# S5 state products alternate over two PSUM rings; tap table stored without gaps from ScalarE's queue

## Chip, core and metric

One core of a Trainium2 chip (trn2) runs the whole program in one launch. The metric is the device time in microseconds; before the change its median over three runs is 2743.06 us (2741.53 to 2747.41). Lower is better.

## What is computed

A two-layer encoder trunk over x of 1 x 1024 x 1024 (time x channels), all in float32. Layer 0 mixes time with RWKV-7, layer 1 with S5, a diagonal complex state space of 64 groups of 16 channels; a squared-ReLU MLP (1024 to 4096 to 1024) follows each, and every sub-layer ends in a layer norm. The part that the change touches is S5:

```python
def s5_mix(x, a_re, a_im, log_dt, b_re, b_im, c_re, c_im, d_skip, w_glu):
    ...
        pr, pi, sr, si = lax.associative_scan(combine, (a_ch_re, a_ch_im, bu_re, bu_im), axis=0)
        carry_re, carry_im = cmul(pr, pi, h_re[None], h_im[None])
        s_re = sr + carry_re
        s_im = si + carry_im
        y = (jnp.einsum('tbgp,gcp->tbgc', s_re, cr_w)
             - jnp.einsum('tbgp,gcp->tbgc', s_im, ci_w))
    ...
    y = jax.nn.gelu(y).astype(x.dtype)
    z = y @ w_glu
    return z[..., :d] * jax.nn.sigmoid(z[..., d:])
```

## The kernel before

Channels lie on partitions (8 tiles of 128), time on the free axis, in two halves of 512 steps, A (time 0 to 511) and B. While one half goes through a mixer, whose work is spread over all engines, the other half's MLP or projections keep PE full: dense products of 128 x 512 (line 188, tile d), three for each weight tile because a float32 weight is split into two reduced parts, whi (ScalarE, line 148) and wlo (VectorE, line 149). A weight block wraw comes by DMA on SyncE's queue (line 169) into two buffers, whi and wlo have three each; one block feeds 12 dense products. A scheduler orders the instructions of each engine by rank and a simulated timeline; on the chip each engine takes them strictly in that order. It also gives every DMA one of eight completion semaphores, in turn and over all queues, so that a DMA whose semaphore is still in use by an earlier one waits for that one to land.

S5 runs in steps of 8 time points. s5_tables (line 1029 on) builds three tables in DRAM, channel tile f by channel tile: tB and tC (input and output of the states), and tT, the taps, by which the 8 inputs of a step act on its 8 outputs directly. For tT, PE makes pk (line 1151), ScalarE copies it into kpad behind eight rows of zeros (line 1155), and SyncE stores eight shifted windows of kpad as one DMA for each parity of the groups (line 1159). kpad's innermost index is the group, so tT's columns have a step of four elements.

s5(H, h) (line 1175 on) then turns each pair f2 of channel tiles (u, pbu), lets VectorE and GpSimd carry the states (advance, hb), and forms the output. For a tile pair it loads tt and tcm for both tiles into four buffers that it shares with tb (lines 1240, 1242), and for each parity of the groups it makes 8 tap products (line 1250: 128 rows, 64 output columns of the array, 128 moving columns) and then 16 state products (line 1255: 64 rows, 64 columns, the two tiles j side by side), all into one bank py of the ring "c" (two buffers):

```python
for par in range(2):
    qs = slice(64 * par, 64 * par + 64)
    p = pc.tile([128, HT], F32, tag="c", name="py").rearrange("p (g n) -> p g n", g=4)
    ...
    S.copy(y1[:, :, :, par].rearrange("p t g c -> p g t c"), p.rearrange("p g (t c) -> p g t c", t=SL))
```

ScalarE copies py to y1 (line 1257), PE turns y1 back (pyt, line 1263, ring "a", two buffers), VectorE adds the skip term (line 1265), ScalarE takes GELU (line 1267) and SyncE stores s_y (line 1268), which the GLU reads again as yl (line 946).

Of the kernel before, what the change touches and what calls it, by code (L numbers as in the profile page):

```python
# [8 lines left out]
F32 = mybir.dt.float32  # L9
# [9 lines left out]
HT = 512  # L19
KT = 8  # L20
# [11 lines left out]
LNT = (2, 5)  # L32
TB = 2
LN8R = 400000
MIXR = 100
# [35 lines left out]
def trunk(ctx, tc, A):  # L71
    nc = tc.nc
    V, S, G, PE, SP = nc.vector, nc.scalar, nc.gpsimd, nc.tensor, nc.sync

    cp = ctx.enter_context(tc.tile_pool(name="cp", bufs=1))
    dr = ctx.enter_context(tc.tile_pool(name="dr", bufs=1, space=DRAM))
# [4 lines left out]
    pl = ctx.enter_context(tc.tile_pool(name="pl", bufs=1, space=PSUM))  # L81
# [80 lines left out]
    def wload(src, kt, n, key=None):  # L162
# [3 lines left out]
        for k0 in range(0, kt, step):  # L166
# [14 lines left out]
            out += [(hi[:, k], lo[:, k]) for k in range(step)]  # L181
        return out

    bulk, hops = [], []
# [835 lines left out]
    SL = 8  # L1020
    NSC = HT // SL
    tT = dr.tile([KT, 128, 2, 512], F32, name="tT")
    tB = dr.tile([KT, 128, 4, 2, 128], F32, name="tB")
    tC = dr.tile([KT, 128, 4, 2, 128], F32, name="tC")

    def s5_tables():
        n = [0]
# [76 lines left out]

        kpad = pp.tile([128, 16, 16, 4], F32, name="kpad")
        G.memset(kpad, 0.0)
        for f in range(KT):
            gs = slice(4 * f, 4 * f + 4)
            bc = pp.tile([128, 2, 2, 4, 16], F32, tag="bc", name="bc", bufs=1)
            SP.dma_start(bc, A["s5bc"][f])  # L1110
# [42 lines left out]
            for par in range(2):  # L1153
                ps_ = slice(64 * par, 64 * par + 16)
                S.copy(kpad[ps_, 8:].rearrange("p t c g -> p g (t c)"), p[ps_])
            tv = tT[f].rearrange("(s c) two n -> two c s n", c=16)
            for par in range(2):
                src = kpad[64 * par : 64 * par + 16, 1:9].rearrange("p t c g -> p (t c g)")
                SP.dma_start(tv[par], bass.AP(src.tensor, src.offset, [src.ap[0], (64, SL), src.ap[1]]))

# [12 lines left out]
    def s5(H, h):  # L1173
# [61 lines left out]
        for f2 in range(4):  # L1235
            y1 = s5p.tile([128, SL, 4, 2, 16], F32, tag="u1", name="y1", bufs=2)
            tabs = []
            for f in (2 * f2, 2 * f2 + 1):
                tt = s5p.tile([128, 2, 512], F32, tag="tab", name="tt", bufs=4)
                SP.dma_start(tt, tT[f])  # L1240
                tcm = s5p.tile([128, 4, 2, 128], F32, tag="tab", name="tcm", bufs=4)
                SP.dma_start(tcm, tC[f])
                tabs.append((f, tt.rearrange("p two (n g) -> p two g n", g=4), tcm))
            for par in range(2):
                qs = slice(64 * par, 64 * par + 64)
                p = pc.tile([128, HT], F32, tag="c", name="py").rearrange("p (g n) -> p g n", g=4)

                for g2 in range(4):
                    for j, (f, tv, tcm) in enumerate(tabs):
                        PE.matmul(p[64 * j : 64 * j + 64, g2], ug[f][:, 2 * g2 + par], tv[:, par, g2],  # L1250
                                  start=g2 == 0, stop=False, skip_group_check=True)
                for g2 in range(4):
                    for ri in range(2):
                        for j, (f, tv, tcm) in enumerate(tabs):
                            PE.matmul(p[64 * j : 64 * j + 64, g2], hb[qs, 4 * f + g2, ri, 0:NSC], tcm[qs, g2, ri],  # L1255
                                      start=False, stop=ri == 1, skip_group_check=True)
                S.copy(y1[:, :, :, par].rearrange("p t g c -> p g t c"), p.rearrange("p g (t c) -> p g t c", t=SL))
            for j in range(2):
                f = 2 * f2 + j
                js = slice(64 * j, 64 * j + 64)  # L1260
                p = pa.tile([128, SL, NSC], F32, tag="a", name="pyt")
                for t in range(SL):
# [133 lines left out]
```

## Time and profile before

| | |
|---|---|
| median of 3 runs | 2743.06 us |
| the profiled execution's own time | 2746.6 us |
| its span | 2744.8 us |
| mean granted TensorE clock | 0.961 of full speed |
| PE / PEld busy | 95% / 76% |
| DVE / ACT / POOL busy | 66% / 42% / 23% |
| chain that ended last | PE 44%, of it line 188 39%; lines 1250 and 1255 1% each |
| S5 tables | about 1100 to 1275 us |
| S5 output of half A / half B | about 1481 to 1540 us / 2010 to 2072 us |

The span is the profiler's time from the first to the last instruction; the execution's own time has the start and the end around it. A busy PE is one with products in flight: products overlap, so what one costs is read from the starts of a group and of the next one, not from its length. Each float32 product here leaves two records in the trace, a dense one of line 188 leaves one.

### The profile page before, as it was taken

Reading aid. Unit: us, or ns where it says so; the run is one execution under the profiler, and the core shown is the slowest. Engines: PE = TensorE matmul, PEld = TensorE weight load, DVE = VectorE, ACT = ScalarE, POOL = GpSimd, SP = SyncE. Lnnn points to the kernel's source line nnn. Section 1 sums busy time; section 2 is a strip of 40 time slices with the busy share of each in tenths; the row PEclk is TensorE's granted clock in tenths of the full one; section 3 lists DMA queues with packets and bytes.
Section 4 is the critical chain, followed back from the end, with each engine's and each line's share of the span. In section 5 each row is a group of like instructions: output and inputs, shape, how many; then the busy total and the mean of one; then the engine's idle time right before and its main releaser. Section 6 shows DMA issues by size and latency. Waiting matters only on the chain.

```text
span 2744.8 us, 43807 instructions
## 1 busy us (share of the span) xinstructions
PE 2598.4 (95%) x16582; PEld 2089.9 (76%) x16582; DVE 1813.3 (66%) x3191; ACT 1154.8 (42%) x2038; POOL 630.6 (23%) x515
## 2 busy tenths in 40 slices
PE   7999979989899999989999999999999999999997
PEld 5778757678677777767876788778778887788886
DVE  7477677577786867997567553674855546755556
ACT  7455574544543333353532332434223324433334
POOL 3121542432442122342122000120220101210101
PEclk9989979999899999999999999999999999999998
DMA  4765455564223334545333533233343322333333
GB/s 146 235 214 175 151 164 156 178 203 142 81 86 88 93 92 148 141 129 163 100 112 127 174 95 100 81 96 112 103 164 110 96 96 81 119 96 96 96 96 100
DMA packets 215058, 345.90 MB, mean 126 GB/s; under 512 B 21184, under 2 KB 75584, under 8 KB 214848
## 3 DMA queue, kind: packets, MB, share of 16 engines
q1 hardware_dynamic: 214848, 343.10, 40.5%
q8 instruction: 131, 2.15, 0.3%
q14 instruction: 79, 0.65, 0.1%
HBM read 279.06 MB, written 63.96 MB: 125 GB/s over the span
## 4 chain that ended last, share of the span: by engine, by line
PE 44%; DVE 4%; issue 3%; DMA 1%; POOL 1%; ACT 1%; ACTq 0%; SPq 0%; DVEq 0%; POOLq 0%
PE d L188 39%; PE py L1250 1%; PE py L1255 1%; DVE wlo L149 1%; DMA wraw<-in_mw_dram 1%; PE pu L154 1%; PE pbu L1206 1%; POOL rl L975 1%; DVE hA L991 0%; DMA s_y<-yg 0%; DVE t L1218 0%; DVE hB L991 0%; ACT whi L148 0%; DVE sq L876 0%; PE pu L1195 0%
## 5 line engine op out<-in xcount | busy, mean ns | idle before, releaser
L148 ACT CAST whi<-wraw 128x512 fp32r<-128x512 f32 x668 | 413.5, 620 | 929.1 <-PE d L188 623.2
L149 DVE TENSOR_TENSOR wlo<-wraw,whi 128x512 fp32r<-128x512 f32 x668 | 500.6, 750 | 426.8 <-ACT whi L148 404.3
L188 PE MATMUL d<-qbuf,whi 128*128 128x512 f32 (+1 forms) x2112 | 657.0, 394 | 23.8 <-DVE hA L991 12.8
L188 PEld LDWEIGHTS d<-qbuf,whi 128*128 128x128 f32 x2112 | 391.8, 191 | 120.0 <-DVE hA L991 17.8
L188 PE MATMUL d<-qbuf,wlo 128*128 128x512 f32 (+1 forms) x1056 | 411.9, 392 | 10.7 <-DVE wlo L149 10.4
L975 POOL TENSOR_TENSOR rl<-rl 128x512 f32<-128x512 f32 x128 | 157.2, 1228 | 1094.5 <-ACT rl L974 1094.5
L188 PE MATMUL d<-oAh,whi 128*128 128x512 f32 (+1 forms) x960 | 390.9, 411 | 15.5 <-ACT ev L418 6.3
L188 PE MATMUL d<-oAl,whi 128*128 128x512 f32 (+1 forms) x960 | 387.5, 405 | 3.0 <-DVE oAl L149 2.8
L188 PE MATMUL d<-oAh,wlo 128*128 128x512 f32 (+1 forms) x960 | 386.5, 405 | 2.4 <-DVE wlo L149 2.3
L188 PE MATMUL d<-oBh,whi 128*128 128x512 f32 x704 | 279.2, 397 | 0.0
L188 PE MATMUL d<-oBh,wlo 128*128 128x512 f32 x704 | 278.7, 396 | 0.2 <-DVE wlo L149 0.2
L188 PE MATMUL d<-oBl,whi 128*128 128x512 f32 x704 | 277.1, 394 | 0.0
L188 PEld LDWEIGHTS d<-qbuf,wlo 128*128 128x128 f32 x1056 | 201.7, 191 | 56.5 <-DVE wlo L149 14.5
L188 PEld LDWEIGHTS d<-oAh,whi 128*128 128x128 f32 (+1 forms) x960 | 185.9, 194 | 62.2 <-ACT ev L418 8.4
L188 PEld LDWEIGHTS d<-oAh,wlo 128*128 128x128 f32 (+1 forms) x960 | 185.8, 194 | 44.4 <-DVE wlo L149 3.2
L188 PEld LDWEIGHTS d<-oAl,whi 128*128 128x128 f32 (+1 forms) x960 | 185.6, 194 | 43.1 <-DVE oAl L149 5.2
L991 DVE TENSOR_TENSOR hB<-hB,d 128x512 f32<-128x512 f32 (+1 forms) x256 | 165.0, 650 | 71.2 <-PE d L188 68.0
L991 DVE TENSOR_TENSOR hA<-hA,d 128x512 f32<-128x512 f32 x240 | 162.1, 682 | 64.4 <-PE d L188 62.1
L188 PEld LDWEIGHTS d<-oBh,wlo 128*128 128x128 f32 x704 | 132.9, 189 | 32.4 <-issue 2.0
L188 PEld LDWEIGHTS d<-oBl,whi 128*128 128x128 f32 x704 | 133.1, 189 | 29.9 <-issue 0.7
L188 PEld LDWEIGHTS d<-oBh,whi 128*128 128x128 f32 x704 | 133.1, 189 | 29.0 <-issue 1.2
L149 DVE TENSOR_TENSOR qbuf<-rl,qbuf 128x512 fp32r<-128x512 f32 x128 | 95.0, 742 | 73.5 <-ACT qbuf L148 73.5
(374 smaller groups left out, 3804.8 us busy)
## 6 DMA issues: line engine op xcount, KB each, us to landing
wraw<-in_mw_dram SPq DMA_DIRECT2D x520, 256.0 KB, 2.7
wraw<-in_glu_dram SPq DMA_DIRECT2D x64, 256.0 KB, 2.7
low<-wlo SPq DMA_DIRECT2D x52, 256.0 KB, 2.6
wlo<-low SPq DMA_DIRECT2D x52, 256.0 KB, 3.6
wraw<-in_wk_dram SPq DMA_DIRECT2D x32, 256.0 KB, 3.5
wraw<-in_wr_dram SPq DMA_DIRECT2D x32, 256.0 KB, 3.9
wraw<-in_wv_dram SPq DMA_DIRECT2D x32, 256.0 KB, 4.3
yl<-s_y SPq DMA_DIRECT2D x32, 256.0 KB, 3.1
```

The lines of the kernel that those rows point to most:

```text
L148: S.copy(hi, src)
L149: (e or V).tensor_sub(lo, src, hi.bitcast(F32))
L154: PE.matmul(out, x, idt, start=True, stop=True)
L188: bulk.append((PE.matmul(p, w, x, **kw).ins, x.shape[-1]))
L975: G.tensor_mul(r, r, r)
L991: V.tensor_add(z, z, p)
L1206: PE.matmul(p[qs, g2, ri], tb[:, g2, ri, qs], u[:, 2 * g2 + par], start=True, stop=True)
L1250: PE.matmul(p[64 * j : 64 * j + 64, g2], ug[f][:, 2 * g2 + par], tv[:, par, g2], start=g2 == 0, stop=False, skip_group_check=True)
L1255: PE.matmul(p[64 * j : 64 * j + 64, g2], hb[qs, 4 * f + g2, ri, 0:NSC], tcm[qs, g2, ri], start=False, stop=ri == 1, skip_group_check=True)
```

## The change

Tap products: all of a tile pair come first, into two banks, one for each parity (ring "c" and ring "a"). State products: the order is now group, part, tile j, parity, and a chain of order-only dependences (inorder) holds it, so that four products in a row use four different quarters of the array and the two parities write different banks. pyt moves to the ring "l" with one buffer. The taps are kept with the time and channel index innermost, in DRAM as well (tT by partition first), so that the table is read without a step. kpad becomes two buffers of four tiles each; after every fourth tile ScalarE's queue starts sixteen stores, one for each of eight time shifts and each parity, whose runs are 128 elements long in kpad and 2048 in DRAM; SyncE's two stores per tile are gone.

```diff
+    def inorder(prods):
+
+        for x, y in zip(prods, prods[1:]):
+            tc.add_manual_dep(y.ins, x.ins.name, mybir.DependencyInfo(
+                mybir.DependencyClass.NoSync, mybir.DependencyReason.DATA), reason="order")
...
-    tT = dr.tile([KT, 128, 2, 512], F32, name="tT")
+    tT = dr.tile([128, 2, KT, 4, 128], F32, name="tT")
...
-        kpad = pp.tile([128, 16, 16, 4], F32, name="kpad")
-        G.memset(kpad, 0.0)
+        kpads = [pp.tile([128, TBF, 4, 16, 16], F32, name=f"kpad{j}") for j in range(KT // TBF)]
+        for kpad in kpads:
+            G.memset(kpad[:, :, :, 0:8], 0.0)
...
-                S.copy(kpad[ps_, 8:].rearrange("p t c g -> p g (t c)"), p[ps_])
-            tv = tT[f].rearrange("(s c) two n -> two c s n", c=16)
-            for par in range(2):
-                src = kpad[64 * par : 64 * par + 16, 1:9].rearrange("p t c g -> p (t c g)")
-                SP.dma_start(tv[par], bass.AP(src.tensor, src.offset, [src.ap[0], (64, SL), src.ap[1]]))
+                S.copy(kpad[ps_, f % TBF, :, 8:].rearrange("p g t c -> p g (t c)"), p[ps_])
+            if f % TBF == TBF - 1:
+                for par in range(2):
+                    for s in range(SL):
+                        S.dma_start(
+                            tT[16 * s : 16 * s + 16, par, f - TBF + 1 : f + 1].rearrange("c f g n -> c (f g) n"),
+                            kpad[64 * par : 64 * par + 16, :, :, 1 + s : 9 + s].rearrange("c f g t e -> c (f g) (t e)"))
...
-                SP.dma_start(tt, tT[f])
+                SP.dma_start(tt.rearrange("p two (g n) -> p two g n", g=4), tT[:, :, f])
...
-                tabs.append((f, tt.rearrange("p two (n g) -> p two g n", g=4), tcm))
+                tabs.append((f, tt.rearrange("p two (g n) -> p two g n", g=4), tcm))
+
+
+            pp = [r.tile([128, HT], F32, tag=t, name="py").rearrange("p (g n) -> p g n", g=4)
+                  for r, t in ((pc, "c"), (pa, "a"))]
+            for g2 in range(4):
+                for par in range(2):
+                    for j, (f, tv, tcm) in enumerate(tabs):
+                        PE.matmul(pp[par][64 * j : 64 * j + 64, g2], ug[f][:, 2 * g2 + par], tv[:, par, g2],
+                                  start=g2 == 0, stop=False, skip_group_check=True)
+            prods = []
+            for g2 in range(4):
+                for ri in range(2):
+                    for j, (f, tv, tcm) in enumerate(tabs):
+                        for par in range(2):
+                            qs = slice(64 * par, 64 * par + 64)
+                            prods.append(PE.matmul(pp[par][64 * j : 64 * j + 64, g2], hb[qs, 4 * f + g2, ri, 0:NSC],
+                                                   tcm[qs, g2, ri], start=False, stop=ri == 1, skip_group_check=True))
+            inorder(prods)
...
-                p = pa.tile([128, SL, NSC], F32, tag="a", name="pyt")
+                p = pl.tile([128, HT], F32, tag="l", name="pyt").rearrange("p (t n) -> p t n", t=SL)
```

On PE, in the S5 output of half A, the second tile pair stood so before (py<-tt are tap products, py<-tcm state products, pyt the transposes of the pair before; the first py<-tt row is already in this order in front of them):

```order
L1250 MATMUL py<-tt,ug 64x128
L1263 MATMUL pyt<-ident,y_13883 128x64 x16
L1250 MATMUL py<-tt,ug 64x128 x7
L1255 MATMUL py<-tcm,hb 64x128 x16
L1250 MATMUL py<-tt,ug 64x128 x8
L1255 MATMUL py<-tcm,hb 64x128 x16
L188 MATMUL d<-oBh,whi 128x512
```

and in the changed kernel so (line numbers of the changed file):

```order
L1280 MATMUL pyt<-ident,y_13901 128x64 x8
L195 MATMUL d<-qbuf,whi 128x512 x2
L195 MATMUL d<-qbuf,wlo 128x512
L195 MATMUL d<-qbuf,whi 128x512
L1262 MATMUL py<-tt,ug 64x128 x14
L1270 MATMUL py<-tcm,hb 64x128
L1280 MATMUL pyt<-ident,y_13901 128x64 x8
L1270 MATMUL py<-tcm,hb 64x128 x31
L1262 MATMUL py<-tt,ug 64x128 x2
L195 MATMUL d<-qbuf,whi 128x512
```

The transposes are in two pieces with the taps between them, and the last two py<-tt belong to the third tile pair: they moved from behind some 24 dense products to the place straight behind this pair's state products. The third pair ends the same way, and half B has the same order.

On ACT, where the last tile's tables are built, this stood before:

```order
L1155 COPY kpad<-pk 16x4x128 x2
L1167 COPY bs<-pb_13342 128x512
L148 CAST whi<-wraw 128x512
L974 ACTIVATE rl<-d 128x512
L148 CAST qbuf<-rl 128x512
L148 CAST whi<-wraw 128x512
L1167 COPY bs<-pb_13348 128x512
L148 CAST whi<-wraw 128x512 x9
```

and now:

```order
L1164 COPY kpad_12866<-pk 16x4x128 x2
L1178 COPY bs<-pb_13360 128x512
L1168 DMA tT<-kpad_12866 16x16x128 x16
L1178 COPY bs<-pb_13366 128x512
L981 ACTIVATE rl<-d 128x512
L149 CAST whi<-wraw 128x512 x2
L149 CAST qbuf<-rl 128x512
L149 CAST whi<-wraw 128x512 x9
```

The sixteen stores stand ahead of one bs copy, one ReLU and all further casts. The fourth tile has the same block of sixteen behind its kpad copies and one cast, ahead of two bs copies and two casts.

## Rows read from the trace of the kernel before

**Rows 1.** The page, part 1: busy time, share of the span, instructions.
```profile
PE 2598.4 (95%) x16582; PEld 2089.9 (76%) x16582; DVE 1813.3 (66%) x3191; ACT 1154.8 (42%) x2038; POOL 630.6 (23%) x515
```

**Rows 2.** Stretches: length; busy us of PE, PEld, DVE, ACT, POOL; clock; DMA share; GB/s.
```profile
1260.00:1280.00 20.00, 19.88 (x114) 15.64 (x113) 15.15 (x25) 8.91 (x14) 2.28 (x2) 1.00 0.66 187
1500.00:1540.00 40.00, 40.00 (x321) 29.94 (x320) 17.97 (x25) 14.48 (x25) 2.09 (x2) 1.00 0.70 246
```

**Rows 3.** Timeline of PE, second tile pair: start us, length us, instruction, count.
```profile
1490.55 2.01 PE L1250 MATMUL py<-tt,ug 128*64 128x128 f32 x14
1492.49 1.96 PE L1255 MATMUL py<-tcm,hb 64*64 64x128 f32 x32
1494.38 2.01 PE L1250 MATMUL py<-tt,ug 128*64 128x128 f32 x16
1496.33 1.96 PE L1255 MATMUL py<-tcm,hb 64*64 64x128 f32 x32
1498.22 0.51 PE L188 MATMUL d<-oBh,whi 128*128 128x512 f32 x1
```

**Rows 4.** Timeline of PE, the products pbu of one channel tile.
```profile
1343.73 2.09 PE L1206 MATMUL pbu<-ug,tb 128*64 128x64 f32 x64
1345.74 0.50 PE L188 MATMUL d<-oBl,whi 128*128 128x512 f32 x1
```

**Rows 5.** Stretches of 0.30 us, line 1255 alone: length, PE busy (records), clock, DMA.
```profile
1482.20:1482.50 0.30, 0.30 (x10) 1.00 0.73 273
1482.88:1483.18 0.30, 0.30 (x16) 1.00 0.20 48
1483.70:1484.00 0.30, 0.30 (x10) 1.00 0.75 273
```

**Rows 6.** Tile py: records, ns min/median/max, first and last start, forms.
```profile
L1255 PE MATMUL py<-tcm,hb x512: 269/269/473, 1481.2 to 2057.2; 64*64 64x128 f32 x171
...
L1250 PE MATMUL py<-tt,ug x256: 388/406/422, 1401.4 to 2055.1; 128*64 128x128 f32 x128
```

**Rows 7.** Timelines of SP and PE, and tile tt: request, next tap product, landing.
```profile
1496.42 0.32 SPq L1240 DMA_DIRECT2D tt<-tT  x1
...
1503.26 0.65 PE L1250 MATMUL py<-tt,ug 128*64 128x128 f32 x2
...
DMA to landing us min/median/max: 3.8/4.2/6.2
```

**Rows 8.** Timelines of PE, DVE and SP: from the transposes to the store of y.
```profile
1489.60 1.01 PE L1263 MATMUL pyt<-ident,y 64*128 64x64 f32 x16
...
1490.35 1.17 DVE L1265 SCALAR_TENSOR_TENSOR yg<-hA,pv,pyt 128x512 f32<-128x512 f32 x1
...
1492.21 0.33 SPq L1268 DMA_DIRECT2D s_y<-yg  x1
```

**Rows 9.** Tile kpad: copies, stores in SP's queue, landing; and SP's timeline.
```profile
L1155 ACT COPY kpad<-pk x16: 1055/1074/1087, 1126.9 to 1267.7; 16x512 f32<-16x512 f32 x16
L1159 SPq DMA_DIRECT2D tT<-kpad x16: 320/362/1264, 1128.6 to 1268.9; - x16
...
DMA to landing us min/median/max: 3.9/4.7/5.8
...
1268.48 0.86 SPq L1159 DMA_DIRECT2D tT<-kpad  x2
```

**Rows 10.** Timelines of ACT and PE at the last tile's tables.
```profile
1268.76 0.59 ACT L1167 COPY bs<-pb 128x512 f32<-128x512 f32 x1
1269.53 0.62 ACT L148 CAST whi<-wraw 128x512 fp32r<-128x512 f32 x1 [0.18 <-PE d L188]
...
1275.49 0.62 PE L188 MATMUL d<-qbuf,whi 128*128 128x512 f32 x2
```

**Rows 11.** Timeline of ACT behind the fourth tile's kpad copies; idle time and releaser.
```profile
1175.73 0.62 ACT L148 CAST whi<-wraw 128x512 fp32r<-128x512 f32 x1 [1.61 <-PE d L188]
```

**Rows 12.** Waits of SP's queue, 1060 to 1300 us: total us, times, longest.
```profile
SPq L1159 <- ACT kpad L1155: 12.4, 8, 4.5
```

More of the change, by code (lines that the diff above doesn't have):

```diff
@@ L33 @@
 TB = 2
+TBF = 4
 LN8R = 400000
@@ L1103, in s5_tables @@
         V.tensor_mul(ci, ci, den)
-        kpad = pp.tile([128, 16, 16, 4], F32, name="kpad")
-        G.memset(kpad, 0.0)
+        kpads = [pp.tile([128, TBF, 4, 16, 16], F32, name=f"kpad{j}") for j in range(KT // TBF)]
+        for kpad in kpads:
+            G.memset(kpad[:, :, :, 0:8], 0.0)
         for f in range(KT):
             gs = slice(4 * f, 4 * f + 4)
+            kpad = kpads[f // TBF]
             bc = pp.tile([128, 2, 2, 4, 16], F32, tag="bc", name="bc", bufs=1)
@@ L1239, in s5 @@
                 tt = s5p.tile([128, 2, 512], F32, tag="tab", name="tt", bufs=4)
-                SP.dma_start(tt, tT[f])
+                SP.dma_start(tt.rearrange("p two (g n) -> p two g n", g=4), tT[:, :, f])
                 tcm = s5p.tile([128, 4, 2, 128], F32, tag="tab", name="tcm", bufs=4)
                 SP.dma_start(tcm, tC[f])
-                tabs.append((f, tt.rearrange("p two (n g) -> p two g n", g=4), tcm))
-            for par in range(2):
[L1245 to L1257, printed above, removed]
@@ L1258, in s5 @@
+            inorder(prods)
+            for par in range(2):
+                S.copy(y1[:, :, :, par].rearrange("p t g c -> p g t c"), pp[par].rearrange("p g (t c) -> p g t c", t=SL))
             for j in range(2):
```

## The prediction

> **What bounds the kernel now.** The page's busy times come first: PE is busy for 95% of the span and every other engine far less [rows 1]. The question for any edit is therefore whether it shortens PE's own stream or makes PE wait. The table of stretches says where: in 1500 to 1540 us, inside the S5 output of the first half, PE is busy for all 40 us at the full clock (the 1.00; 2.4 GHz), while DVE has 18.0 us and ACT 14.5 us of work, and the DMA engines are 70% busy with 246 GB/s [rows 2]. There a microsecond less of PE work is a microsecond less of time, unless something PE reads comes later than before. In 1260 to 1280 us, where the last tables are built, PE is busy for 19.88 of 20 us as well [rows 2], so a delay on ACT there is not free.
>
> The timeline of PE inside one pair of channel tiles then gives prices as start-to-start times, which is what counts, because the products overlap: a row's own length (406 or 269 ns each) is not its cost. Eight pairs of tap products (16 records, since each product leaves two) take 1494.38 to 1496.33, 1.95 us; sixteen pairs of state products (32 records) take 1492.49 to 1494.38 and again 1496.33 to 1498.22, 1.89 us each [rows 3]. So a tap pair costs 0.244 us and a state pair 0.118 us, switching included, though both stream 128 columns.
>
> **The change, part by part.**
>
> *Tap products, contiguous table.* They read the moving operand with a step of four elements (16 bytes) before, and without a gap after. The trace has the same tile form without a gap in the products pbu: 128 rows by 64 columns, two at a time, 64 moving columns; 64 records, so 32 pairs, go from 1343.73 to 1345.74, 0.063 us a pair [rows 4]. Twice the columns is 0.126 us, against 0.244. There are 256 records [rows 6], so 128 pairs, in 16 groups of eight: 1.95 less 8 x 0.126 = 0.95 us each, **15.2 us** in all. Bounds: 0, if the step is not why they are slow, and 15.2. I take 15.2, since pbu differs from them in the step and the length alone. The Trainium skill ("SBUF — State Buffer", "Door 1: The DMA port swizzle") says that memory is read in lines of 16 bytes, that full speed wants two hits on a line, and then that one can step freely over "4 fp32". Its first half makes this step slow, its second makes it free; by the second the taps would gain 0 and the sum below would be -2.4 us.
>
> *State products, four in a row.* Before, a parity's 16 pairs run on one half of the array's rows; now the parities alternate, each with a bank of its own. The trace shows four at once by accident: in the first tile pair the two parities' groups follow each other directly, and where the second starts while the first drains, 0.30 us holds 16 records, against 10 in the stretches before and behind it, with records of the same length [rows 5]. 512 records [rows 6] are 16 groups of 1.89 us, 30.2 us; half is 15.1, less about 1 for that overlap, which exists already twice: **14 us**. Bounds: 0 and 15.1. I take 14, because in rows 5 both streams keep their own pace.
>
> *Table loads (a wait added).* All four tables of a tile pair share four buffers, so the next tap table is asked for when the last tap product of this one is done (before: 1496.42, behind the taps that end at about 1496.3) and lands 4.2 us later, 6.2 at most [rows 7]. Before, dense products filled that time and the next tap product started at 1503.26 [rows 7]. Now two tap products of the next pair stand straight behind this pair's state products, at two places in each half, and everything behind them on PE waits with them. Between request and use lie 32 state products (about 1.0 us at four in a row, and some 0.35 us of switching), and half the transposes with their switching (0.8 us): with the tail of the taps about 2.7 us. Wait: 4.2 - 2.7 = 1.5 us, four times, **+6 us**. Bounds: 0 (the request is early) and 4 x (6.2 - 2.7) = 14. At the first of these places the store of y stands ahead of the request on SP; it began 2.6 us after the transposes did (1489.60 to 1492.21) [rows 8], about when the taps now end, so it adds nothing.
>
> *Denser traffic.* The 9.8 MB of 1500 to 1540 us [rows 2] would pass in some 29 us, since three tile pairs of that stretch lose 29.2 / 8 = 3.65 us each: 0.70 x 40 / 29 is 0.97 of the DMA engines. Loads will land later. I put **+4 us**, between 0 and 10 (the 2.0 us by which the slowest table load lies above the median, at each of five loads).
>
> *Stores in ACT's queue.* Sixteen stores follow each other after every fourth tile. On SP two took 0.86 us [rows 9], so sixteen take 6.9 us, in which ACT casts nothing. The second burst: the copies into kpad now write runs without a gap, which I price as the bs copy, 0.59 us [rows 10] for 1.07 [rows 9], so that the bs copy of 1268.76 ends near 1268.4. Behind the burst come a bs copy, a ReLU and the cast, 1.8 us, and the cast of 1269.53 serves the tile that PE begins at 1275.49 [rows 10]: cover 5.3 us, **+1.6 us**. The first burst stands ahead of the cast of 1175.73, which had waited for PE to free a buffer [rows 11], so three tiles of 2.7 us lie ahead of it: 0. Bounds: nothing for 0.32 us a store, and 26 us in all for 1.26 [rows 9]; I take 0.43, the nearest row. The hb memset and the tb loads that wait for the last stores fall into the same cover. SP loses 16 issues and the 12.4 us it waited for kpad [rows 12], which lets weights come sooner; in stretches where PE waits for little, 0.
>
> *Nothing for* the wider memsets (POOL is 77% idle [rows 1]), the moved copies, and the second transposes in the one "l" bank: they start some 2.4 us behind the first, whose reader on DVE takes 1.17 us [rows 8]. If DVE is late, that is at most one more such reader at each of six places, 7 us.
>
> **Sum:** -15.2 - 14 + 6 + 4 + 1.6 = -17.6 us. The profiled execution took 2746.6 us, 3.5 above the median 2743.06, so 2729 there and **2726 us** as a median.
>
> **Rivals.**
> - *The tables set the pace.* For: 0.97 of the DMA engines, four waits in PE's order. Against: dense products still lie between most loads and uses. Waits at their upper bound of 14 and 2 more for traffic: -7.6, 2735 us.
> - *Nothing new waits.* Then -29, 2714 us. Against it stands the order itself.
> - *The taps stay slow* (two streams from 128 rows hold each other up at this length, or the step is free, the skill's second half). For: no row has 128 columns without a step in this form. -2.4, 2741 us.
> - *Four in a row don't run at once* in the steady state. For: rows 5 are one short overlap. -3.6, 2739 us.
> - *The bursts cost more than the products give: slower.* Eight completion semaphores serve all DMAs in turn, so a store may wait for the one eight ahead of it. If a store lands L us after its issue, each costs L/8, and both bursts together 32 x L/8 less the cover of 5.3 and 9: the gain of 19.2 that is left is gone at L = 8.4. kpad's stores landed in 4.7, 5.8 at most [rows 9], but with runs four times as long; at 10 us and with the weight loads that share these semaphores late by as much again, about 9 us slower, 2752 us.
>
> **How the numbers follow.** Forecast 0.55 (with its unknowns 2719 to 2733), tables set the pace 0.17, nothing waits 0.07, taps stay slow 0.08, no four at once 0.07, bursts 0.06. The range 2713 to 2741 leaves out the bursts and the edges of the others. Within 0.2% (5.5 us, about what a measurement can tell) lie the taps and the four-at-once rivals, 0.15; slower 0.06; faster 0.79.
>
> **What would show it.** Tap products at about 270 ns each instead of 406, eight pairs in about 1.0 us; state records of 269 ns with four starts per 0.11 us; PE idle 1 to 2 us before the two early tap products; a gap of about 7 us on ACT at each burst, with PE short of a cast behind the second. The forecast is wrong if tap products stay at 406 ns, if PE's wait at the tables passes 3 us at each place, or if a burst holds ACT for more than 10 us.

## The result and the profile after

The changed kernel takes 2754.78 us (median of 11 runs, 2742.77 to 2758.5) against 2741.53 us for the kernel before (11 runs beside it): ratio 1.0049, 95% interval 1.0036 to 1.0063. It is **slower by half a per cent**; the forecast was 2726 us, so faster. 2754.8 also lies outside the stated range of 2713 to 2741.

Part 1 of the page, and its row on ScalarE's DMA queue:

```profile
PE 2576.1 (94%) x16582; PEld 2078.5 (75%) x16582; DVE 1823.6 (66%) x3191; ACT 1145.2 (42%) x2038; POOL 643.0 (23%) x516
...
q10 hardware_dynamic: 8704, 4.20, 1.1%
```

PE is busy 22.3 us less than before [rows 1] and the span is 8.7 us longer (2753.5 against 2744.8): the work did shrink, and PE stood idle 31 us more. Where, the stretches say (columns as in rows 2):

```profile
1260.00:1280.00 20.00, 16.44 (x98) 12.58 (x97) 10.72 (x16) 4.00 (x7) 1.51 (x1) 1.00 0.62 134
1280.00:1300.00 20.00, 11.17 (x38) 9.01 (x39) 7.03 (x12) 3.97 (x7) 1.04 (x1) 0.66 0.80 196
1500.00:1540.00 40.00, 34.35 (x395) 27.80 (x394) 15.96 (x19) 13.87 (x24) 3.09 (x2) 0.96 0.76 256
```

Two places that were full before [rows 2] have holes: the end of the tables, where PE does 27.6 us of work in 40 and the granted clock falls to 0.66 in the second half, and the S5 output, where PE is idle for 5.65 of 40 us.

**The tables.** Timeline of ACT at the second burst (ACTq are the DMA issues in its queue):

```profile
1267.66 1.18 ACT L1164 COPY kpad<-pk 16x512 f32<-16x512 f32 x2 [0.75 <-PE pk L1160]
1268.26 1.62 ACTq L1168 DMA_DIRECT2D tT<-kpad  x2
1268.86 0.59 ACT L1178 COPY bs<-pb 128x512 f32<-128x512 f32 x1
1269.91 17.23 ACTq L1168 DMA_DIRECT2D tT<-kpad  x14
1287.18 0.59 ACT L1178 COPY bs<-pb 128x512 f32<-128x512 f32 x1 [17.74 <-DMA tT<-kpad]
...
1288.15 1.14 ACT L149 CAST whi<-wraw 128x512 fp32r<-128x512 f32 x2
```

Sixteen stores last from 1268.26 to 1287.14, and only then come the second bs copy and the casts that PE needs. PE's timeline and one stretch of it show what that costs:

```profile
1288.83 2.93 PE L195 MATMUL d<-qbuf,whi 128*128 128x512 f32 x6 [12.39 <-ACT whi L149]
1291.55 0.63 PE L195 MATMUL d<-qbuf,wlo 128*128 128x512 f32 x1
...
1294.79 0.61 PE L195 MATMUL d<-qbuf,whi 128*128 128x512 f32 x2
1295.24 0.39 PE L195 MATMUL d<-qbuf,wlo 128*128 128x512 f32 x1
```

```profile
1280.00:1294.00 14.00, 5.17 (x12) 0.51 0.77 144
```

PE waits 12.39 us for the first cast. And the wait costs more than its length: from 1280 to 1294, within the wait and for five us behind it, the granted clock is 0.51, so at the lower of its two levels (1.2 GHz), and the first six products behind the wait take 0.45 us each (1288.83 to 1291.55), against 0.23 at full clock (1294.79 to 1295.24). The tile's view gives the price of one store, and the chain of work that ended last, cut to 1260 to 1300 us, shows that they are the path:

```profile
L1168 ACTq DMA_DIRECT2D tT<-kpad x32: 348/1259/2462, 1170.1 to 1285.6; - x32
L1164 ACT COPY kpad<-pk x16: 570/577/579, 1125.9 to 1268.3; 16x512 f32<-16x512 f32 x16
...
DMA to landing us min/median/max: 2.9/5.3/7.3
```

```profile
by line: ACTq L1168 43.7%; PE d L195 28.9%; DMA wraw<-in_mw_dram 16.0%; issue 5.8%; PE pk L1160 5.0%; DVE wlo L150 1.7%; ACT bs L1178 1.5%; ACT whi L149 1.3%; ACT rl L981 1.2%; ACT kpad L1164 1.0%; DVE hA L998 0.1%; DVEq L150 0.1%
```

A store takes 1.26 us (median), not 0.43. The kpad copy, 1074 ns before [rows 9], takes 577, as the prediction had it.

**The S5 output.** Tap products and state products in the tile's view and in PE's timeline (half A, pairs two and three):

```profile
L1262 PE MATMUL py<-tt,ug x256: 272/273/475, 1417.5 to 2061.0; 128*64 128x128 f32 x128
```

```profile
1506.15 3.38 PE L1262 MATMUL py<-tt,ug 128*64 128x128 f32 x28 [3.86 <-DMA tt<-tT]
...
1510.46 1.97 PE L1270 MATMUL py<-tcm,hb 64*64 64x128 f32 x62
...
1519.76 1.96 PE L1262 MATMUL py<-tt,ug 128*64 128x128 f32 x28
1521.65 0.86 PE L1270 MATMUL py<-tcm,hb 64*64 64x128 f32 x18
```

Fourteen tap pairs take 1519.76 to 1521.65, 0.135 us each (0.244 before, 0.126 forecast), and 62 state records take some 1.9 us, where 32 did [rows 3]: both products are as fast as forecast. But PE stands still in front of them, and behind the wait of 3.86 us the same 28 tap records take 3.32 us (1506.15 to 1509.47): the granted clock is 0.55 there. Its waits in 1465 to 1560 us (total us, times, longest):

```profile
PE py L1262 <- DMA tt<-tT: 5.2, 3, 3.9
PE d L195 <- DVE hB L998: 3.4, 4, 1.4
PE d L195 <- ACT rl L981: 2.5, 2, 1.6
PE pyt L1280 <- DVE hb L1189: 1.5, 1, 1.5
```

Lining up the 544 additions of tile d that VectorE makes to hA and hB in both traces tells how the difference grew: +0.8 us at 1274, +16.1 at 1289, +14.7 at 1488, +10.2 at 1556, +15.1 at 1985, +10.9 at 2060, +7.7 at the end. The second burst costs 15 us at one stroke, and the two outputs give back 4 to 5 us each, where some 14 were forecast for each before its waits.

Cutting both traces at the same additions gives an account by stage. "Clock" is an estimate of what the low clock costs: half of PE's busy time in the stretches in which the granted clock is 0.50.

| stage, by the times of the trace before | before, us | after, us | difference | PE idle more | clock |
|---|---|---|---|---|---|
| end of the tables, 1255 to 1310 | 64.8 | 80.6 | +15.8 | +12.4 | +2.6 |
| S5 output of half A and around it, 1410 to 1560 | 140.5 | 133.4 | -7.1 | +8.1 | -1.4 |
| S5 output of half B and around it, 1930 to 2090 | 159.5 | 156.8 | -2.7 | +9.3 | +1.5 |
| everything else | 2380.0 | 2382.7 | +2.7 | +1.1 | +2.9 |

In the two outputs, then, PE's work fell by some 27 us, near the 29.2 that was forecast, and 17.4 us of new idle time took most of it back.

### The profile page after: what moved, and what is told of

Read it like the earlier page. It is cut to its first block, busy times and chain, and to the rows that moved or that the text cites. A ratio compares the mean times of both kernels' runs of the same rounds, so it can differ in the third digit from the quotient of the medians.

```text
span 2753.5 us, 43797 instructions
## 1 busy us (share of the span) xinstructions
PE 2576.1 (94%) x16582; PEld 2078.5 (75%) x16582; DVE 1823.6 (66%) x3191; ACT 1145.2 (42%) x2038; POOL 643.0 (23%) x516
## 4 chain that ended last, share of the span: by engine, by line
PE 60%; DVE 14%; DMA 9%; issue 8%; ACT 5%; POOL 3%; ACTq 1%; SPq 0%; DVEq 0%; POOLq 0%
PE d L195 52%; DVE wlo L150 3%; PE pA L603 1%; ACTq L1168 1%; DMA s_y<-yg 1%; DMA wraw<-in_mw_dram 1%; DMA yl<-s_y 1%; POOL rl L982 1%; ACT whi L149 1%; DMA ldsg<-s_sg 1%; DVE hA L998 1%; DMA s_r<-ev 1%; PE pbu L1217 1%; PE pu L155 1%; DVE sq L883 1%
## 5 line engine op out<-in xcount | busy, mean ns | idle before, releaser
L150 DVE TENSOR_TENSOR wlo<-wraw,whi 128x512 fp32r<-128x512 f32 x668 | 512.0, 768 | 413.8 <-ACT whi L149 391.6
L195 PE MATMUL d<-qbuf,whi 128*128 128x512 f32 (+1 forms) x2112 | 658.0, 395 | 41.3 <-ACT whi L149 13.2
L982 POOL TENSOR_TENSOR rl<-rl 128x512 f32<-128x512 f32 x128 | 161.6, 1263 | 1111.5 <-ACT rl L981 1111.5
```

The lines of the kernel that those rows point to most:

```text
L150: (e or V).tensor_sub(lo, src, hi.bitcast(F32))
L195: bulk.append((PE.matmul(p, w, x, **kw).ins, x.shape[-1]))
L982: G.tensor_mul(r, r, r)
```

## The experiments

The theory after the first reading: the bursts cost the time, and the products gain what was forecast less the table waits. Its rival: the product block or the table loads cost it, and the bursts are harmless. A second question was open from the start: whether a burst costs because of the queue it stands in, the many short runs, the bytes, or the number of stores. All ratios are to the kernel before, run on the same chip beside each batch (its medians there were 2739.0 to 2741.3 us).

| run | edit | us, median | ratio, 95% interval |
|---|---|---|---|
| the change | | 2754.8 | 1.0049, 1.0036 to 1.0063 |
| e1 | its stores from SP | 2755.0 | 1.0058, 1.0035 to 1.0081 |
| e11 | its table, stored tile by tile | 2739.9 | 0.9995, 0.9984 to 1.0007 |
| e20 | its bursts, runs of 2 KB | 2751.2 | 1.0039, 1.0017 to 1.0061 |
| e22 | the same, stores of 64 KB | 2752.5 | 1.0048, 1.0032 to 1.0064 |
| e3 | products alone | 2743.4 | 1.0015, 0.9996 to 1.0034 |
| e6 | taps alone, no burst | 2728.7 | 0.9960, 0.9945 to 0.9975 |
| e7 | both, no burst | 2736.5 | 0.9988, 0.9974 to 1.0001 |
| e10 | e7, stores from ACT | 2734.2 | 0.9981, 0.9970 to 0.9991 |
| e8 | e7, pyt in the ring of two | 2736.2 | 0.9994, 0.9978 to 1.0010 |
| e9 | e7, yg in a shared ring | 2872.3 | 1.0488, 1.0464 to 1.0511 |
| e12 | e8, y stored by ACT | 2743.2 | 1.0010, 0.9997 to 1.0023 |
| e13 | e6, y stored by ACT | 2738.0 | 0.9992, 0.9975 to 1.0009 |
| e14 | e12, both tt loaded first | 2745.6 | 1.0020, 1.0006 to 1.0034 |
| e15 | e7, y stored by ACT | 2739.4 | 1.0008, 0.9988 to 1.0027 |
| e16 | e8, y written over ug | 2726.8 | 0.9956, 0.9938 to 0.9974 |
| e17 | e7, y written over ug | 2732.3 | 0.9970, 0.9956 to 0.9983 |
| e18 | e6, y written over ug | 2731.5 | 0.9968, 0.9949 to 0.9987 |
| e23 | e16, tables before yl | 2725.0 | 0.9956, 0.9942 to 0.9969 |

### What the bursts cost

**e1: the same stores from SP.**

```
-                        S.dma_start(
+                        SP.dma_start(
                             tT[16 * s : 16 * s + 16, par, f - TBF + 1 : f + 1]...
```

> The changed kernel with its 32 stores issued by SyncE in place of ScalarE, nothing else. Theory (the loss is ScalarE's queue: stores of 1.1 to 1.3 us each stand ahead of the casts that PE waits for): ScalarE's bs copies start at once, the second burst's 16 us come back, and the kernel falls from 2754.8 to about 2739, unless SP's weight loads are now held up by the same 20 us per burst, in which case it stays at 2750 to 2760 and the price belongs to the stores and not to the queue. Rival (table loads and product order cost the time, bursts are harmless): 2755 as it was.

2755.0 us, no change. SP's timeline shows the second burst, and the waits of PE in 1160 to 1320 us what stands behind it:

```profile
1268.55 3.46 SPq L170 DMA_DIRECT2D wraw<-in_mw_dram  x2
1272.38 19.46 SPq L1168 DMA_DIRECT2D tT<-kpad  x16
1291.93 1.27 SPq L1179 DMA_DIRECT2D tB<-bs  x1
```

```profile
PE d L195 <- ACT whi L149: 23.9, 2, 13.8
```

Sixteen stores last 19.5 us in SP's queue, about as in ACT's (20.5 and 18.9). Now no weights are asked for meanwhile, and PE waits 23.9 us for casts (13.2 in the changed kernel, where PE waits 8.2 us more for a bs copy behind the first burst). ScalarE's queue is acquitted; whoever issues the burst is shut for it. This agrees with the first half of what the Trainium skill says ("DMA: Bandwidth & Descriptors", "Issuing engines are not separate DMA queues"), that DMAs of different engines run on the same DMA engines in the end; that the time to begin a DMA is usually small beside the DMA does not hold for this shape, 1.26 us against 5.3 to the landing.

**e11: the same table, eight stores of 64 KB per tile.**

```
-            if f % TBF == TBF - 1:
...
+            for par in range(2):
+                for g in range(4):
+                    src = kpad[64 * par : 64 * par + 16, f % TBF, g, 1:9].rearrange("p t c -> p (t c)")
+                    SP.dma_start(tT[:, par, f, g].rearrange("(s c) n -> c s n", c=16),
+                                 bass.AP(src.tensor, src.offset, [src.ap[0], (16, SL), src.ap[1]]))
```

> The changed kernel with its contiguous table of 512-byte runs stored tile by tile from SyncE: eight stores of 64 KB per tile, 64 in all, in place of two bursts of 16 of 128 KB. Same bytes and same runs, spread over eight tiles. Theory (the burst, not the layout, cost 16 to 18 us): each set of eight fits between the tiles at 0.3 to 0.7 us a store, and the time falls to that of e7, 2735 to 2742. Rival (short runs cost wherever they stand): 39 us of stores hold SP's weight loads, and it stays at 2750 to 2760.

2739.9 us: the same runs of 512 bytes and the same 4.2 MB, not gathered, and 15 us are back. Its view of kpad:

```profile
L1168 SPq DMA_DIRECT2D tT<-kpad x64: 326/430/1326, 1128.0 to 1267.7; - x64
```

Note that the issues still take 31 us of SP in all (sum of the 64 records); they lie in eight pieces between other loads, where PE does not feel them.

**e10: stores of 256 KB from ACT.** Meant as two bursts of eight with runs of 2 KB, on top of e7.

```
-        kpad = pp.tile([128, 16, 4, 16], F32, name="kpad")
+        kpads = [pp.tile([128, TBF, 16, 4, 16], F32, name=f"kpad{j}") for j in range(KT // TBF)]
...
+            if f % TBF == TBF - 1:
+                for x in range(TBF):
...
+                        S.dma_start(tv[par], bass.AP(src.tensor, src.offset, [src.ap[0], (64, SL), src.ap[1]]))
```

> e7 with its 16 stores held back and begun by ScalarE in two bursts of eight after tiles 3 and 7, as in the changed kernel, but with runs of 2 KB: 256 KB and 128 runs each, so the same bytes as the changed kernel's burst (2 MB) in a quarter of the runs. If each of the many short runs costs (about 5 ns, 1.3 us per 256): eight stores last about 5 us and the kernel stays at 2736 to 2742. If bytes cost (1.3 us per 128 KB): eight stores last about 19 us again, ScalarE is shut for them, and the kernel is back at 2750 to 2756.

2734.2 us, but it doesn't answer that question. A store here needs one tile only, and the scheduler sent each pair behind its tile: the sixteen issues start at 1124, 1141, 1152 and so on to 1263, and take 7.5 us in all. What it does show is that stores in ACT's queue are harmless when they are few and spread.

**e20: the held burst with longer runs.** Every store again needs all four tiles, so the burst can't be pulled apart.

```
-        kpads = [pp.tile([128, TBF, 4, 16, 16], ...
+        kpads = [pp.tile([128, TBF, 16, 4, 16], ...
...
-                            kpad[64 * par : 64 * par + 16, :, :, 1 + s : 9 + s].rearrange("c f g t e -> c (f g) (t e)"))
+                            kpad[64 * par : 64 * par + 16, :, 1 + s : 9 + s].rearrange("c f t g e -> c f (t g e)"))
```

> The changed kernel with the rows of its table in the order t, g, c, so that each of its 32 stores (same two bursts after tiles 3 and 7, ScalarE's queue, 128 KB each) has 64 runs of 2 KB in place of 256 of 512 bytes; a store still needs all four tiles, so a burst cannot be pulled apart. If runs cost (1.3 us per 256): stores take 0.35 to 0.5 us, a burst lasts 6 to 8 us, and the kernel falls to 2737 to 2742. If bytes cost (1.3 us per 128 KB): the burst stays at 17 to 20 us and the kernel at 2750 to 2756.

2751.2 us. ACT's timeline at the second burst, and the tile's view:

```profile
1263.63 1.65 ACTq L1168 DMA_DIRECT2D tT<-kpad  x2
...
1265.31 16.46 ACTq L1168 DMA_DIRECT2D tT<-kpad  x14
```

```profile
L1168 ACTq DMA_DIRECT2D tT<-kpad x32: 356/1272/2234, 1165.6 to 1280.5; - x32
```

A quarter of the runs, the same 1.27 us: runs are not the price.

**e22: half as large stores.**

```
-                        S.dma_start(
...
+                        for x in range(0, TBF, 2):
+                            S.dma_start(
+                                tT[16 * s : 16 * s + 16, par, f - TBF + 1 + x : f - TBF + 3 + x], ...
```

> e20 with each store of the bursts cut in two by tiles: 32 stores of 64 KB (32 runs of 2 KB) per burst in place of 16 of 128 KB, same bytes, same bursts after tiles 3 and 7. If bytes set the pace (128 KB per 1.27 us, some 100 GB/s): 0.6 to 0.7 us each, a burst still lasts 17 to 20 us, 2748 to 2756. If each store costs its 1.27 us whatever its size: a burst lasts 40 us, and the kernel goes to 2765 to 2785.

2752.5 us, in the range for bytes, but the time doesn't decide it. The scheduler sent the first half of each burst two tiles earlier, so there are four bursts of 1 MB. The second and the last of them in ACT's timeline, and the tile:

```profile
1176.48 12.67 ACTq L1169 DMA_DIRECT2D tT<-kpad  x16
...
1257.01 8.65 ACTq L1169 DMA_DIRECT2D tT<-kpad  x16
```

```profile
L1169 ACTq DMA_DIRECT2D tT<-kpad x64: 309/442/1858, 1146.9 to 1265.2; - x64
```

Sixteen stores take 12.67 and 8.65 us, not 20, so it isn't a price per store. It isn't simply one per byte either: half the bytes cost a third (0.44 us against 1.27, medians). In e1 the first three stores of a burst take 0.42 to 0.63 us each and most of the rest 1.0 to 1.7; in the last burst here the first eight take 4.45 us and the last eight 4.20, without such a step. Nor does the prediction's own mechanism, eight completion semaphores in turn, explain it: at 1.27 us a store, the store eight places ahead was begun ten us earlier and had landed after 5.3 (7.3 at most), so no store waited for it. Why stores of 128 KB from 16 partitions, sixteen in a row, come to 1.27 us each, 103 GB/s, stays open.

The time of e22 isn't the price of its bursts alone. In its trace the stage from 1150 to 1310 us is 7.2 us longer than before, where the changed kernel's is 16.6 longer; the stages of the two S5 outputs are 8.8 us longer than the changed kernel's, though the edit doesn't touch them.

### What the products gain

**e6: taps alone.** A layout (t, g, c) keeps SP's two stores per tile as they were, and the taps read runs of 16 elements.

```
-        kpad = pp.tile([128, 16, 16, 4], F32, name="kpad")
+        kpad = pp.tile([128, 16, 4, 16], F32, name="kpad")
...
-                tabs.append((f, tt.rearrange("p two (n g) -> p two g n", g=4), tcm))
+                tabs.append((f, tt.rearrange("p two (t g c) -> p two g t c", t=SL, g=4), tcm))
```

> The kernel before with another table layout alone (t, g, c in place of t, c, g), so that the taps read runs of 16 elements in place of single elements 16 bytes apart; SyncE's two stores per tile, of runs of 2 KB, stay, and so does the order of the products. Theory: runs of 16 are read as fast as a whole row, tap products fall from 400 to 270 ns each and 16 groups of eight pairs give 15 us: 2726 to 2731. Rival (only a wholly contiguous row is read at full rate, or the strided step is free and something else made the taps faster): 2741 as before.

2728.7 us: faster by 0.40%, 11 us (7 to 15). PE's timeline in the second pair, to set beside rows 3:

```profile
1483.51 1.96 PE L1255 MATMUL py<-tcm,hb 64*64 64x128 f32 x32
1485.40 1.09 PE L1250 MATMUL py<-tt,ug 128*64 128x128 f32 x16
1486.43 1.96 PE L1255 MATMUL py<-tcm,hb 64*64 64x128 f32 x32
```

Eight tap pairs take 1.03 us instead of 1.95: 16 x 0.92 = 14.7 us of work. Runs of 16 are enough. Of the two halves of the Trainium skill's note on memory lines that the prediction weighed ("SBUF — State Buffer", "Door 1: The DMA port swizzle"), the first holds here and the second, as the prediction read it, does not: a step of four fp32 is not free, 406 ns a record against 273.

**e3: products alone.** The diff is the product block of the change and its pyt line, on the kernel before.

> The kernel before with the product block alone: state products four in a row, two rings for the accumulators, the third for pyt; strided table and SyncE's two stores per tile stay. Theory: 16 groups of 32 products give 14 us, less some 3 to 6 us for table loads that come later: 2727 to 2733, against 2741.5 before. Rival (the product block is what made the changed kernel slow): 2745 to 2755.

2743.4 us, between the ranges of the theory and of the rival: nothing gained, where 14 us were forecast. **e7: both, without bursts** (e3's block on e6's layout).

> The table layout and the product block together, with SyncE's two stores per tile as before: the change without its bursts. Theory: the two gains add to 20 to 29 us, less 4 to 9 for table loads that come late: 2715 to 2725, some 35 below the changed kernel. Rival (table loads set the pace once products are short): 2735 to 2742.

2736.5 us, where its rival had it. With the products in a row the median is 0.28% (8 us) *above* e6, though PE has less to do; the intervals only just touch. So the change seems to have two faults, and the second was hidden under the first. For the S5 outputs the trace gives this, from the first state product of a half to its last transposes; idle is the sum of the gaps between PE's records, clock the mean granted one:

| kernel | half A: us, idle, clock | half B: us, idle, clock | dense records inside, each half |
|---|---|---|---|
| before | 52.4, 0.0, 1.00 | 52.4, 0.0, 0.99 | 78 |
| the change | 55.7, 8.3, 0.97 | 56.6, 7.8, 0.94 | 102 |
| e6 | 46.7, 1.0, 1.00 | 54.4, 2.4, 0.87 | 78 |
| e3 | 57.3, 4.8, 0.97 | 57.6, 5.0, 0.97 | 102 |
| e7 | 58.4, 9.6, 0.94 | 55.1, 7.4, 0.97 | 102 |
| e8 | 47.1, 6.7, 0.93 | 47.9, 7.5, 0.89 | 78 |
| e16 | 43.3, 4.9, 0.96 | 48.4, 8.3, 0.87 | 78 |
| e23 | 38.3, 1.3, 1.00 | 43.8, 6.5, 0.96 | 78 |

Each dense record more is 0.23 us of other work that fell inside. The clock matters as much as the idle time: e6 has the same work in both halves, but in half B, behind a wait of 2.09 us for a table, the granted clock is 0.52 for 14 us:

```profile
2018.00:2032.00 14.00, 14.00 (x91) 0.52 0.63 210
```

PE is busy throughout and half B is 7.7 us longer. Each row is one execution, so such a stretch is part of the scatter.

e3 leaves PE idle for 9.8 us where it was never idle before, so some 10 of the 14 went into waits; 6.9 us of its waits are for tables. The waits of DVE and of PE in e7 (1470 to 1550 us) name three kinds:

```profile
DVE yg L1276 <- DMA s_y<-yg: 14.0, 3, 7.2
```

```profile
PE pyt L1274 <- DVE hb L1184: 3.3, 1, 3.3
PE py L1256 <- DMA tt<-tT: 3.2, 2, 1.8
...
PE pyt L1274 <- DVE yg L1276: 2.0, 2, 1.3
```

DVE reads pyt into the single buffer yg, gelu works on it, SP stores it, and only when the store has landed may the next read begin. PE's transposes wait for that read, since pyt has one bank. The table loads stand in SP's queue behind the same stores and, the first of them, behind weight loads.

**e8: pyt back in the ring of two.**

```
-                  for r, t in ((pc, "c"), (pa, "a"))]
+                  for r, t in ((pc, "c"), (pc, "c"))]
...
-                p = pl.tile([128, HT], F32, tag="l", name="pyt").rearrange("p (t n) -> p t n", t=SL)
+                p = pa.tile([128, HT], F32, tag="a", name="pyt").rearrange("p (t n) -> p t n", t=SL)
```

> e7 with the banks given out as in the kernel before: both accumulators from the ring of two called c, pyt back in the ring of two called a, products still four in a row. Theory (the short products lose their gain because pyt has one bank: its second set waits for VectorE's first read, and that for the store of the single yg buffer): e7's 17 us of idle PE in the two stretches fall to 3 to 6 (table loads stay), and the time from 2736.5 to 2718 to 2726, below e6's 2728.7. Rival (table loads that come late are what the products run into): the waits on tt grow by what pyt no longer takes, and the time stays at 2733 to 2738, above e6.

2736.2 us, as the rival said. The waits of pyt on DVE are gone and those on the tables grew (same window):

```profile
PE py L1256 <- DMA tt<-tT: 5.1, 2, 3.4
PE pyt L1274 <- ACT y L1268: 1.6, 1, 1.6
```

**e9: three buffers for yg, from a ring that others use.**

```
-                y = s5p.tile([128, HT], F32, tag="yg", name="yg", bufs=1)
+                y = tp.tile([128, HT], F32, tag="ev", name="yg", bufs=3)
```

> e7 with yg taken from a ring of three buffers that relu and gate tiles also use, pyt still in its one bank. Theory (the single yg buffer, held for 2.8 us by the store, is the second half of the pyt chain): VectorE's 3.3 to 7.2 us waits on the store go and 3 to 7 of e7's 17 us of idle PE with them: 2729 to 2734. If the one bank alone is to blame: 2736.5 as e7. If the shared ring makes relu wait: above 2738.

2872.3 us, and it tells nothing of yg. The S5 output of half A starts at 1388 us (1471 in e7), with no dense product inside it, and PE waits 37.4 us for hb: with the shared ring the scheduler's whole order came out otherwise.

**e12 to e15: y stored by ACT**, behind its own gelu, to free SP's queue for the tables.

```
-                SP.dma_start(scr["y"][f * 128 : ...
+                S.dma_start(scr["y"][f * 128 : ...
```

> e8 with the stores of y (s_y<-yg) begun by ScalarE right behind its gelu, nothing else moved by hand. Theory (e8's tt waits of 3.4 and 3.9 us come from SP's queue: the second table load of a pair stands behind the y store, which waits for gelu, and behind the yl load, which waits for that store): the table requests move up by 2 to 4 us, the 10.6 us of waits on tt fall under 5, and the time from 2736.2 to 2727 to 2731. Rival (the table waits for its buffer, which the pair before frees too late, and SP's order is no part of it): 2734 to 2738.

> e12 with the four loads of a pair in another order: both tt, then both tcm, so that the two tt take the buffers that the pair before frees after its taps. Theory (buffers come free too late for the second tt): waits on tt vanish, another 3 to 5 us below e12, 2722 to 2728. Rival (tcm then comes late and the state products wait for it instead): no change from e12, within 3 us.

> e6 (new table layout, old product order) with the stores of y begun by ScalarE. Its PE idles only 3.4 us in the two stretches, so theory gives at most 2 to 3 us: 2725 to 2729. If 16 stores of 0.3 to 0.4 us in ScalarE's queue cost more than they give: 2730 to 2735.

> e7 (pyt in its one bank) with the stores of y begun by ScalarE. If SP's queue is what holds the tables and the yg buffer, e7's waits on tt and part of its pyt waits go: 2726 to 2732. If the one bank is what counts, 2733 to 2738 as e7.

All four medians lie above those without it, by 3 to 9 us (e14 2 above e12); e13's interval just touches e6's, the others overlap with theirs. In e12 the tables do come in time, and another wait takes their place (PE, 1470 to 1550 us):

```profile
PE pyt L1274 <- ACT y L1268: 6.8, 1, 6.8
PE py L1256 <- ACT y L1268: 4.1, 1, 4.1
```

ACT's queue runs in order. Its copies of the accumulators stand behind a gelu, and the gelu behind DVE's read, which waits for the landing of the store before (DVE's waits on s_y<-yg over the whole program: 34.0 us, 16.2 in e8). Moving one member of a ring of waits to another queue did not open the ring; loading both tt first (e14) did not either.

**e16 to e18: y written over ug**, whose eight buffers are dead once the pair's taps are done.

```
-                y = s5p.tile([128, HT], F32, tag="yg", name="yg", bufs=1)
+                y = ug[f].rearrange("p g n -> p (g n)")
```

> e8 with y written over ug[f] (dead after its pair's taps, eight buffers) in place of the single yg buffer; stores of y back in SP's queue. Theory (with short products the y chain sets the pace: read of pyt 1.1 us, gelu 0.6, store and its landing about 3, all through one buffer, eight times per half): VectorE's 16 us of waits on s_y go, table requests no longer stand behind late y stores, idle PE of the two stretches falls from 14 to under 6 us: 2718 to 2727. Rival (table loads, by buffers): tt waits stay at 10 us and the time at 2733 to 2738.

> e7 (pyt in its one bank) with y written over ug[f]. Theory: the first read no longer waits for a store, so the one bank costs only the read itself; pyt waits fall from 8 to under 4 us and the time from 2736.5 to 2720 to 2730. If the one bank alone is to blame: 2733 to 2738.

> e6 (new table layout, old product order) with y written over ug[f]. PE waits for little there, so the chain has room: 2726 to 2730, within 3 us of e6. If it gains more than 4 us, the yg chain was already at the end of the path with long state products, against the theory.

On e8 it gives 0.38%, some 10 us, and the intervals are apart. But the traces don't place this gain in the outputs. DVE's waits for y's stores are gone, as meant; PE's idle time in the two outputs is 13.2 us, 14.2 in e8, where under 6 was expected; and of the 9.0 us between the two profiled executions 7.3 lie in the first 1000 us, which the edit doesn't touch. So that the single yg buffer costs time is not shown. On e6 the edit gives nothing (2731.5 against 2728.7, intervals overlap); PE idles little there without it. On e7, with one bank for pyt, it gives 4 us, which the intervals don't separate from none. First among the things that PE waits for in e16 is a table (1470 to 1550 us):

```profile
PE py L1256 <- DMA tt<-tT: 4.9, 2, 3.8
```

In SP's queue the second tap table of that pair stands behind two loads of yl, which wait for the landing of y's stores.

**e23: the tables before yl.**

```
-            SP.dma_start(y, scr["y"][k * 128 : ...
+            q = SP.dma_start(y, scr["y"][k * 128 : ...
+            if last[0] is not None:
+                inorder([last[0], q])
...
-                SP.dma_start(tcm, tC[f])
+                last[0] = SP.dma_start(tcm, tC[f])
```

> e16 with the loads of y for the gate (yl<-s_y) put behind the last table load of the half in SP's queue, since e16's largest waits on tt (3.75 and 5.61 us) stand behind two yl loads that wait 3.4 us for the landing of their stores. Theory: those two waits go, up to 9 us, and ScalarE's casts of yl no longer hold the copies of the accumulators: 2718 to 2724. Rival (the gate's products then start late, or the tables wait for buffers): 2725 to 2732.

The waits on tt fall to 0.9 and 1.4 us, and the two outputs to 82.1 us from 104.8 before. PE's work in them (time less idle) is 74.3 us against 104.8: 30.5 us less, so the 29.2 that the prediction counted for both products were really there. The time is 2725.0 us, at the lower end of the rival's range, 0.44% below the kernel before, below the changed kernel by 0.9%, and not apart from e16 or e6: with these repairs the products in a row add at most a few us to what the taps alone gave. In half B, 5.1 us of waiting for ACT's copy of y remain.

## Why the prediction was wrong

- **The step that failed first: stores in ACT's queue**, +1.6 us. It priced a store at the 0.43 us of two stores on an empty queue [rows 9] and took sixteen for 6.9 us. They last 19 to 20.5 us. The 1.26 us named there as a bound is what came (median 1.26): the row existed, and the nearer one was taken as typical. A row of two issues says nothing on the sixteenth. The cost in time is 15 us (against e11) to 17 us (against e7). In the trace the second burst makes it at one stroke: 12.4 us of PE waiting for a cast, and some 2.6 us of low clock behind the wait, a term that the prediction doesn't have. "The forecast is wrong if a burst holds ACT for more than 10 us" was the right test.
- **The rival that ended slower** was right in its place and nearly in its time (2752 against 2754.8), the latter by luck: its mechanism is not what happened, since the stores landed in 5.3 us, not 10, and none waited for the one eight ahead. Its chance of 0.06 was far too low for a term whose own bounds reached 26 us.
- **The step that failed second: the waits that the shorter products run into**, +6 for tables and +4 for traffic. State products, -14 us, run four in a row as forecast, but e3 gains nothing. In the two outputs of the changed kernel PE's work fell by some 27 us, and its idle time grew by 17.4 us instead of 10. Tables are 9.9 of it, near the 10. The rest the prediction put at nothing: dense products that wait for DVE's additions and ACT's ReLU, transposes that wait for y and hb. It treated PE's saved time as saved as long as tables arrive; before, PE never stood still in the outputs; with some 14 us less of work in each it did. Which of these waits costs how much is not shown: e8 and e16 took some away and others grew; only e23 brings the idle time of both outputs down to 7.8 us, and its time is not apart from e6.
- **Tap products**, -15.2 us: right. 14.7 us of work, and 11 us (7 to 15) of time in e6.
- **Table loads**, +6 us: 9.9 us of PE's waits on tt in the two outputs (5.2 in half A, 4.7 in half B), within the bounds of 0 and 14, but the sum behind the 6 was wrong. It took the 32 state products of a tile pair for 1.0 us; by its own rows 16 take 1.89 us, and half of that when four run at once, so 32 take 1.9, as they did; the wait then comes to 0.6 us at each of four places, 2.4 in all, and +6 came nearer by luck. The places were partly others: the largest, 3.86 us, comes from a request at 1500.06 that stood in SP's queue behind weight loads. **Denser traffic**, +4: landings of tt rose by 0.3 us only (4.2 to 4.5), and the DMA share in 1500 to 1540 us is 0.76, not 0.97; those 40 us have holes of PE in them.
- **The one "l" bank**, at most 7 us, taken as nothing: right as far as e8 against e7 can tell.
- **The first burst**, 0 us: it lasts 20.5 us, from 1170.1 to 1190.6, and PE waits 8.2 us for a bs copy behind it; but PE had waits there before as well, so it costs 2 us by the alignment, some 4 against e7's. The cover of 9 us that the prediction counts for it is not worked out there (three tiles of 2.7 us are 8.1).

Put together from runs: both products without bursts are worth 3 us (e7, its interval just reaches none), the bursts cost 15 to 17, and the change is 13 us slower.

## What to carry to other kernels

Price a run of DMA issues by its last one, not by its first: the rows of a lone pair hide what a queue does when it is full, and gathering stores that were spread between tiles can cost more than the work they serve. Before shortening the products of the bounding engine, follow what they read to the queue it stands in and each result to where its buffer comes free again: what the long products covered turns into waits. Count such a wait at more than its length; here the granted clock stood at half behind the longer ones. And test each part of a change alone: here one part was worth 11 us, and the whole lost 13.

## What the runs showed of the hardware

- Stores of 128 KB from 16 partitions, sixteen in a row, take 1.26 to 1.33 us to issue (medians; the first three of a burst in e1 0.42 to 0.63), alike from SP (e1) and from ACT, and alike with 256 runs of 512 bytes and 64 runs of 2 KB (e20). Stores of 64 KB take 0.44 (e22), and sixteen in a row 8.65 and 12.67 us.
- Products with a moving operand of eight runs of 16 elements (e6) take 273 ns a record, the same as with whole rows of 128; with single elements 16 bytes apart 406.
- State products of alternating row halves and two banks start 62 records in some 1.9 us, 0.061 us a pair, against 0.118 in rows 3.
- In a wait of PE of 12.39 us and for five us behind it, from 1280 to 1294, the granted clock was 0.51; the dense products behind the wait took 0.45 us each, 0.23 at full clock (the change). Behind one of 2.09 us it was 0.52 for 14 us (e6, half B), with PE busy throughout.
